# A two-layer diffusion block in fp32 on one core: GpSimd's sums go to VectorE and ScalarE, one-hots are built by fours, and the ordering pass gets new costs and slot rules

## The chip, the cores and the metric

The kernel runs on one core of a Trainium2 chip. The metric is the device time of one execution in microseconds (us), as the median of several runs. The engines are written as the profile writes them: PE (TensorE matmul), PEld (its weight loads), DVE (VectorE), ACT (ScalarE), POOL (GpSimd), SP (SyncE, which here only issues DMAs).

## The reference, cut to what matters

Two layers work on 256 latent tokens and 256 context tokens of width 1024. Each layer has a token mixer with three branches and then a feed-forward that picks 128 of 16384 experts for each token.

```python
def token_mixer(h, hc, ...):          # latent and context tokens
    qA, kA, vA, qB, kB, vB, qkvC, zC, aC, bC, gl = split_cols(h @ w_in)
    oA, oAc = diff_attention(...)     # softmax attention, difference of two maps
    oB, oBc = window_gqa(...)         # windowed attention with a sink
    oC, oCc = gated_deltanet(...)     # chunked recurrence, forward and backward
    return merge_branches((oA, oB, oC), gl, b_gate, w_branch, w_out), ...

def peer_ffn(h, wq, keys, u_tab, v_tab):
    q = (t @ wq).reshape(n, 8, 2, 128)
    s = einsum('thcd,cnd->thcn', q, keys)
    sv, si = top_k(s, 16)                          # of 128, per half
    cand = sv[:, :, 0, :, None] + sv[:, :, 1, None, :]
    cv, ci = top_k(cand, 16)                       # 16 of the sums
    eid = i1 * 128 + i2;  gw = softmax(cv)
    act = gelu(einsum('pd,ped->pe', t, u_tab[eid]))
    return einsum('pe,ped->pd', act * gw, v_tab[eid])

for l in range(2):
    m, mc = token_mixer(...)
    x = x + gt1 * m
    x = x + gt2 * peer_ffn(modulate(x, ...), ...)
    if l == 0:                                     # the context ends after layer 0
        xc = xc + gt1c * mc
        xc = xc + gt2c * peer_ffn(modulate(xc, ...), ...)
```

## The kernel before

The program isn't written in the order in which it runs. `Kern` calls methods of `Rec`, which looks like the five engines and only records operations (`Op`). `Rec.order` then plays a list schedule: it has a duration for each operation (`cost`), a priority (the place in the recording plus `base`), and pools of SBUF and PSUM slots, and it writes down in which order each engine gets its instructions. `emit` issues them in that order, so that all instructions stand at one line of the profile (L603), and groups are told apart by operation, names and shapes. Each engine then runs its own list in order.

**Slots.** Working tiles live in classes: `b4` (4 KB a partition, 36 slots), `b2` (9), `b1` (8), and 8 PSUM banks `ps`. Three tags have no slots of their own and borrow them (`BORROW`): `rows` up to 8 of `b4` and `ga` up to 3 of `b4` for the gathers below, `psg` up to 2 of `ps`. `restore` gives them back. Before the change it runs when a tile of that very tag is freed and the gathers' list is already done; the last `rows` tile is freed ahead of the list's end, the last `ga` tile at its end.

**Lanes and distance.** The gathers are recorded in lane -1, all else in lane 0. An operation that opens a tile may run ahead of the oldest unfinished one by a weighted amount of work `FAR`, and from `NEAR` on it must leave `SPARE` slots of each class free.

**Splits.** A product in fp32 accuracy is three fp32r matmuls (`mm3`): each operand is split into a rounded part (`scalar.copy`, shown as ACT CAST) and a rest (a subtraction, shown as TENSOR_TENSOR fp32r<-f32, on DVE or POOL). `WPOOL` sends half of the weight pieces of layer 0's latent mixer to POOL, `UP1` every fourth of the first 64 `u` chunks' splits of layer 1, and `VP = 8` seven of eight `v` splits of layer 1.

**Stages.** Labels are layer and stream: `01` is layer 0's context, `00` its latents, `11` and `10` the same for layer 1. In the order of time: `01` mixer; `01 front` and `01 route` (top-k of the experts, a long run of DVE instructions); then side by side the `00` mixer and the context's expert layer by gathers (`peer_gather`): `U0`, `V0`, `U1`, `V1` for the two blocks of 128 tokens. A `U` step is an indirect DMA on POOL that fetches 128 rows of 4 KB into a `rows` tile, and a DVE product with a sum (SCALAR_TENSOR_TENSOR rows<-rows,ga); a `V` step is four such DMAs and eight small matmuls. The latents' expert layer runs densely (`peer_dense`): `route`, then `build`, which makes for each token a 128x128 matrix of weights from two one-hot matrices and one matmul and stores it to HBM, 16 tokens at a time; then for each of the 128 chunks of 128 experts `dU` (24 matmuls of 256 columns, GELU) and `dV` (12 matmuls of 512 columns). `pre` is the number of `dU` chunks that are recorded ahead of the first `dV`. Layer 1 follows: `11` mixer, `10` mixer, `10 route`, `10 build`, `10 dU` and `10 dV`.

`Kern.aux` is the engine of three kinds of products in `route` (sums of candidates, and two products in `decode`): DVE in layer 0, POOL in layer 1. In the recurrence (`gdn_chains`) POOL multiplies masks and rows by a gate for each of two heads at once: `m1`, `m2` (names consts, gd_g), `vb` (gd_hb), `kd` (gd_ex), `kg` (gd_bg).

Of the kernel before, what the change touches and what calls it, by code (L numbers as in the profile page):

```python
# [20 lines left out]
KT = 8  # L21
# [22 lines left out]
WPOOL = (1, 3, 5, 7)  # L44
UP0, UP1 = (), range(0, 64, 4)
PRE1 = 64
OUTV = False
# [3 lines left out]
VP = 8  # L51
GBASE, RBASE = 0, -8000
PRE = 48
LOAD = {"tensor": 1.0, "vector": 0.3, "scalar": 0.2}
NEAR, FAR = 20.0, 150.0
# [224 lines left out]
class Rec:  # L280
# [5 lines left out]
    def __init__(self, nc, pools, bufs):  # L286
# [5 lines left out]
        self.lane, self.cw = 0, {}  # L292
# [8 lines left out]
    def cost(self, eng, meth, out, ins, kw, args):  # L301
# [27 lines left out]
        if kw.get("op") == OP.pow:
            return 0.3 + 0.165 * n, 0  # L330
        c = {"tensor_tensor": 2.2, "memset": 0.3, "tensor_copy": 3.6}.get(meth, 4.0)
        return 0.05 + n * c / 1000.0, 0

    def add(self, eng, meth, args, kw):
# [10 lines left out]
        o.dur, o.dma = self.cost(eng, meth, outs[0], ins, kw, args)  # L345
        preds = {}
# [23 lines left out]
        o.lane = self.lane  # L370
        o.cw = self.cw[o.lane] = self.cw.get(o.lane, 0.0) + o.dur * LOAD.get(eng, 0.0)
# [14 lines left out]
    def order(self):  # L386
# [55 lines left out]
        together, last_out, pe_at = {}, None, 0.0  # L442
# [13 lines left out]
        def borrow(tag):  # L456
# [4 lines left out]
            if not slots[a] or load[a][ops_at(owner[a]):].max(initial=0) > cap[a] - 1:  # L461
# [15 lines left out]
        def blocked(o):  # L477
            for t in o.tiles:
# [1308 lines left out]
```

## Time and profile before

| | |
|---|---|
| three runs | 3962.46, 3938.74, 3939.72 us |
| median | 3939.72 us |
| the profiled execution | 3933.92 us, of which its span 3932.1 us |
| mean granted TensorE clock | 0.933 of 2.4 GHz |
| busy, share of the span | PE 90%, PEld 76%, DVE 63%, ACT 41%, POOL 38% |
| HBM | 837.78 MB by DMA, 213 GB/s in the mean |

The span runs from the program's first instruction to its last. Matmul ends are modelled and matmuls overlap, so a busy PE isn't a PE at its peak, and PE's share alone doesn't say what a stage costs. Shares are means over stages with different limits; the stretches below are cut at the stages.

### The profile page before, as it was taken

Reading aid. Unit: us, or ns where it says so; the run is one execution under the profiler, and the core shown is the slowest. Engines: PE = TensorE matmul, PEld = TensorE weight load, DVE = VectorE, ACT = ScalarE, POOL = GpSimd, SP = SyncE. Lnnn points to the kernel's source line nnn. Section 1 sums busy time; section 2 is a strip of 40 time slices with the busy share of each in tenths; the row PEclk is TensorE's granted clock in tenths of the full one; section 3 lists DMA queues with packets and bytes.
Section 4 is the critical chain, followed back from the end, with each engine's and each line's share of the span. In section 5 each row is a group of like instructions: output and inputs, shape, how many; then the busy total and the mean of one; then the engine's idle time right before and its main releaser. Section 6 shows DMA issues by size and latency. Waiting matters only on the chain. (4 is left out here: it accounts for less than half of the span.)

```text
span 3932.1 us, 64402 instructions
## 1 busy us (share of the span) xinstructions
PE 3530.0 (90%) x24312; PEld 2982.5 (76%) x24312; DVE 2472.8 (63%) x5599; ACT 1610.0 (41%) x3070; POOL 1481.9 (38%) x1125
## 2 busy tenths in 40 slices
PE   7999964986997798889999999998996899899999
PEld 6787954866794467767777888877896699678998
DVE  4444579889656886897444454646559942555554
ACT  4544422433442233343333346544543343344443
POOL 1110123778364345663333202222023043675443
PEclk9999986877898999999999998988998999999999
DMA  7356742566466799999889851302351455565653
GB/s 279 112 169 239 254 168 98 184 230 233 161 206 231 252 368 376 384 409 361 334 332 333 310 195 43 103 28 89 103 197 65 129 184 170 190 222 213 221 207 142
DMA packets 300966, 837.78 MB, mean 213 GB/s; under 512 B 26736, under 2 KB 96752, under 8 KB 300656
## 3 DMA queue, kind: packets, MB, share of 16 engines
q1 hardware_dynamic: 153168, 522.80, 37.2%
q0 software_dynamic: 73728, 268.47, 18.6%
q10 hardware_dynamic: 73760, 42.40, 3.6%
q8 instruction: 192, 3.15, 0.3%
q14 instruction: 118, 0.97, 0.1%
HBM read 792.67 MB, written 40.89 MB: 212 GB/s over the span
## 5 line engine op out<-in xcount | busy, mean ns | idle before, releaser
L603 PE MATMUL ps<-b,b 128*128 128x256 f32 (+4 forms) x18528 | 2742.4, 309 | 202.7 <-DVE b L603 134.8
L603 PEld LDWEIGHTS ps<-b,b 128*128 128x128 f32 (+2 forms) x18528 | 2449.7, 192 | 476.8 <-DVE b L603 163.3
L603 DVE TENSOR_TENSOR b<-b,b 128x1024 fp32r<-128x1024 f32 (+3 forms) x1065 | 1142.8, 1106 | 817.2 <-ACT b L603 550.9
L603 ACT CAST b<-b 128x1024 fp32r<-128x1024 f32 (+1 forms) x982 | 917.4, 976 | 702.6 <-PE ps L603 297.9
L603 POOL TENSOR_TENSOR b<-b,b 128x1024 fp32r<-128x1024 f32 (+2 forms) x241 | 586.8, 2445 | 922.7 <-DVE b L603 367.5
L603 ACT COPY b<-ps 128x256 f32<-128x256 f32 (+3 forms) x896 | 291.2, 350 | 676.4 <-PE ps L603 666.6
L603 POOL DMA_INDIRECT rows<-in_u_tab,eid x256 | 357.8, 1398 | 271.1 <-DVE rows L603 118.2
L603 POOL DMA_INDIRECT rows<-in_v_tab,eidT x256 | 284.0, 1109 | 426.5 <-PE ps L603 354.6
L603 PE MATMUL ps<-b 128*128 128x128 f32 (+1 forms) x2048 | 337.9, 320 | 19.2 <-ACT b L603 7.5
L603 PE MATMUL ps<-consts,b 128*128 128x128 f32 (+1 forms) x1290 | 261.1, 316 | 103.8 <-DVE b L603 76.9
L603 ACT ACTIVATE b<-ps 128x512 f32<-128x512 f32 (+1 forms) x264 | 136.7, 520 | 523.5 <-PE ps L603 507.0
L603 PEld LDWEIGHTS ps<-b 128*128 128x128 f32 (+1 forms) x2048 | 255.7, 207 | 119.6 <-DVE b L603 39.6
L603 DVE SCALAR_TENSOR_TENSOR rows<-rows,ga 128x1024 f32<-128x1024 f32 x256 | 322.9, 1288 | 4.4 <-DMA rows<-in_u_tab,eid 2.4
L603 PEld LDWEIGHTS ps<-consts,b 128*128 128x128 f32 x1290 | 184.4, 180 | 148.2 <-issue 68.8
L603 DVE TENSOR_SCALAR b<-consts,b 128x128 f32<-128x128 f32 x1024 | 235.4, 309 | 10.8 <-DMA gd<-b 7.7
L603 PE MATMUL ps<-rows,ga 128*32 128x512 f32 x1024 | 160.5, 626 | 19.0 <-DMA rows<-in_v_tab,eidT 17.8
L603 DVE COPY_PREDICATED b<-masks,ps 128x64 f32<-128x64 uint8 (+1 forms) x416 | 83.7, 251 | 148.5 <-PE ps L603 146.9
L603 ACT COPY b<-b 128x128 f32<-128x128 f32 x384 | 108.0, 303 | 60.5 <-DVE b L603 56.1
L603 DVE TENSOR_TENSOR b<-ps,b 128x128 f32<-128x128 f32 (+4 forms) x144 | 61.9, 454 | 93.8 <-PE ps L603 57.8
L603 PEld LDWEIGHTS ps<-rows,ga 128*32 128x32 f32 x1024 | 29.5, 111 | 94.6 <-DMA rows<-in_v_tab,eidT 47.8
L603 PE MATMUL ps<-b,cs 128*32 128x256 f32 x768 | 69.8, 430 | 12.2 <-DVE cs L603 11.5
L603 ACT ACTIVATE b<-b 128x512 f32<-128x512 f32 (+1 forms) x62 | 38.9, 629 | 96.0 <-DVE b L603 42.5
(176 smaller groups left out, 1450.6 us busy)
## 6 DMA issues: line engine op xcount, KB each, us to landing
b<-in_u_cols SPq DMA_DIRECT2D x256, 512.0 KB
b<-in_v_tab SPq DMA_DIRECT2D x256, 512.0 KB
b<-in_w_in SPq DMA_DIRECT2D x184, 512.0 KB
gd<-b ACTq DMA_DIRECT2D x64, 512.0 KB
b<-gd SPq DMA_DIRECT2D x64, 512.0 KB
b<-in_w_ada SPq DMA_DIRECT2D x48, 512.0 KB
b<-in_w_ada SPq DMA_DIRECT2D x96, 256.0 KB
b<-in_wq SPq DMA_DIRECT2D x48, 512.0 KB
```

The lines of the kernel that those rows point to most:

```text
L603: r = getattr(getattr(nc, o.eng), o.meth)(*[_real(x) for x in o.args], **{k: _real(x) for k, x in o.kw.items()})
```

## The change

Constants: `WPOOL`, `UP1` become empty and `VP` 1, so that no split is on POOL; `OUTV` sends the output projection's sum to DVE, and `aux` stays DVE in layer 1. The sum in `qk_prep` goes from POOL to DVE. The five gate products of `gdn_chains` become ScalarE activations with a scale pointer, one a head. In `weights` four tokens' first one-hots are one DVE TENSOR_TENSOR with broadcast operands, and of each four second one-hots one is made by ScalarE as relu(gw - gw * |i - iota|). `order` gives all borrowed slots back when the gathers' list is done, lets `rows` borrow with a look only as far as the place where the two lists meet, has `FAR` at 80 for 150, `pre` at 32 for 48 in layer 0, leaves routing out of the distance (`URGENT = 0`), and lets layer 1's context mixer run ahead of `FAR` once the gathers are done (`FREE1`). Its cost table has new numbers, and two instructions of DVE and POOL that both read two SBUF tensors can't start at one time in its play (`port`).

```diff
-WPOOL = (1, 3, 5, 7)
-UP0, UP1 = (), range(0, 64, 4)
+WPOOL = ()
+UP0, UP1 = (), ()
-OUTV = False
+OUTV = True
-VP = 8
+VP = 1
+ACTB = (1, 1)
+TAIL, FREE1 = 0, True
+FREE = {"b4": 4, "b2": 2, "b1": 1, "ps": 0}
-PRE = 48
+PRE = 32
-NEAR, FAR = 20.0, 150.0
+NEAR, FAR, URGENT = 20.0, 80.0, 0.0
...
+        o.port = eng in ("vector", "gpsimd") and not o.dma and sum(
+            isinstance(x, V) and x.n > 1 and x.tile.kind == "sb" for x in ins) > 1
...
+                    if o.port:
+                        at = max(at, port)
+                        port = at + o.dur
...
-                if t.tag in BORROW and (not BORROW[t.tag][2] or lpos[lane] == len(lanes[lane])):
-                    restore(t.tag)
+                for tag in BORROW:
+                    if owner.get(tag) == lane and (lpos[lane] == len(lanes[lane]) or tag == t.tag and not BORROW[tag][2]):
+                        restore(tag)
...
-            nc.gpsimd.tensor_tensor(qv, qv, t1, op=OP.add)
+            nc.vector.tensor_tensor(qv, qv, t1, op=OP.add)
...
-                nc.gpsimd.tensor_tensor(m1, M1[:, None, :].to_broadcast([P, H2, P]), bc(gc), op=OP.mult)
+                for h in range(H2):
+                    nc.scalar.activation(m1[:, h], M1, AF.Copy, scale=gc[:, h:h + 1])
...
+                nc.vector.tensor_tensor(A[:, :, 0], io4, sc[:, 1, k:k + 4, None].to_broadcast([P, 4, P]), op=OP.is_equal)
                 for t in range(4):
                     k = t0 + q + t
-                    nc.vector.tensor_scalar(A[:, t, 0], self.iota, sc[:, 1, k:k + 1], None, OP.is_equal)
-                    nc.vector.tensor_scalar(A[:, t, 1], self.iota, sc[:, 0, k:k + 1], sc[:, 2, k:k + 1],
-                                            OP.is_equal, OP.mult)
+                    if t >= ACTB[l]:
+                        nc.vector.tensor_scalar(A[:, t, 1], self.iota, sc[:, 0, k:k + 1], sc[:, 2, k:k + 1],
+                                                OP.is_equal, OP.mult)
+                    else:
+                        d = A[:, t, 1]
+                        nc.scalar.activation(d, self.iota, AF.Abs, scale=-1.0, bias=sc[:, 0, k:k + 1])
+                        nc.scalar.activation(d, d, AF.Relu, scale=sc[:, 3, k:k + 1], bias=sc[:, 2, k:k + 1])
...
-        self.aux = self.nc.gpsimd
+        pass
         self.lab("1 norm1")
+        self.nc.free = FREE1
```

The change moves instructions between engines and lets the play order all of them anew. On PE the list stays close: it has the same 20928 operations, and most stages begin within some 250 places of where they began (`00 dV` and `V1` some 350 to 400 places earlier).

**POOL in the `00` mixer, beside the gathers.** In the list before, gate products of the recurrence and a weight split (the 128x1024 row) stand between the gathers' DMAs (`rows<-in_u_tab`):

```order
L603 TENSOR_TENSOR b_1647_8025<-consts_71,gd_g_7192 128x256 x2
L603 TENSOR_TENSOR b_1575_7605<-b_1468_7506,gd_hb_7171 128x256
L603 TENSOR_TENSOR b_1611_7699<-b_1467_7461,gd_bg_7252 128x256
L603 TENSOR_TENSOR b_1575_7605<-b_1467_7461,gd_ex_7241 128x256
L603 COPY b_1646_8070<-consts_71 128x256
L603 TENSOR_TENSOR b_1956_8086<-consts_71,rows_p_91 128x128 x2
L603 DMA rows_8097<-in_u_tab,eid_1303_6473 128x1024
L603 TENSOR_TENSOR b_1611_7699<-b_1468_7506,gd_hb_7171 128x256
L603 DMA rows_8117<-in_u_tab,eid_1303_6473 128x1024
L603 TENSOR_TENSOR b_1611_7699<-b_1467_7461,gd_ex_7241 128x256
L603 TENSOR_TENSOR b_1689_8137<-b_1687_7398,b_1688_7580 128x1024
L603 DMA rows_8165<-in_u_tab,eid_1303_6473 128x1024
```

In the list after, the same stretch of POOL has the DMAs and a few small rows:

```order
L625 DMA rows_8252<-in_u_tab,eid_1303_6459 128x1024
L625 DMA rows_8277<-in_u_tab,eid_1303_6459 128x1024
L625 DMA rows_8295<-in_u_tab,eid_1303_6459 128x1024
L625 COPY b_1732_8316<-consts_71 128x256
L625 TENSOR_TENSOR b_1865_8334<-consts_71,rows_p_91 128x128 x2
L625 DMA rows_8347<-in_u_tab,eid_1303_6459 128x1024
L625 DMA rows_8376<-in_u_tab,eid_1303_6459 128x1024
```

The gate products now stand on ACT between the recurrence's copies, two for each that POOL had. On DVE, 81 of the 128 sums of `U0` stand ahead of the first instruction of `00 attB1`, where 112 stood; 5 stand ahead of the end of `01 route`, where 13 stood.

**DVE and ACT in `10 build`.** DVE had eight one-hots for four tokens, on its list before:

```order
L603 TENSOR_SCALAR b_5907_31178<-consts_71,b_5777_30336 128x128 x8
L603 TENSOR_SCALAR b_5909_31196<-consts_71,b_5777_30336 128x128 x8
L603 TENSOR_SCALAR b_5911_31214<-consts_71,b_5777_30336 128x128 x8
L603 TENSOR_SCALAR b_5913_31230<-consts_71,b_5777_30336 128x128 x8
L603 TENSOR_SCALAR b_5917_31246<-consts_71,b_5777_30336 128x128 x8
```

and has four instructions for them after:

```order
L625 TENSOR_TENSOR b_5831_30687<-consts_71,b_5781_30474 128x4x128
L625 TENSOR_SCALAR b_5831_30687<-consts_71,b_5781_30474 128x128 x3
L625 TENSOR_TENSOR b_5833_30703<-consts_71,b_5781_30474 128x4x128
L625 TENSOR_SCALAR b_5833_30703<-consts_71,b_5781_30474 128x128 x3
L625 TENSOR_TENSOR b_5835_30727<-consts_71,b_5781_30474 128x4x128
```

ACT had the two copies out of PSUM for each four tokens and the two stores for each sixteen. After, the fourth one-hot's two activations stand among them, one or two groups of four ahead of the copies:

```order
L625 DMA gd_30575<-b_5809_30646 1024x1x128
L625 DMA gd_30577<-b_5810_30651 1024x1x128
L625 ACTIVATE b_5831_30687<-b_5831_30687,b_5781_30474 128x128
L625 ACTIVATE b_5833_30703<-consts_71,b_5781_30474 128x128
L625 COPY b_5819_30706<-ps_30691 128x64x4
L625 COPY b_5820_30711<-ps_30691 128x64x4
L625 ACTIVATE b_5833_30703<-b_5833_30703,b_5781_30474 128x128
L625 COPY b_5819_30706<-ps_30708 128x64x4
L625 COPY b_5820_30711<-ps_30708 128x64x4
```

**POOL in layer 1's expert layer.** Its list before has 144 splits of `u` and `v` tiles here, and ends with these rows:

```order
L603 TENSOR_TENSOR b_6969_37880<-b_6967_37776,b_6968_37871 128x1024
L603 TENSOR_TENSOR b_6972_37898<-b_6970_37794,b_6971_37877 128x1024
L603 TENSOR_TENSOR b_6985_37924<-b_6983_37828,b_6984_37906 128x1024
L1783 UNCONDITIONAL_BRANCH
L1783 ISA
```

After, its last work is the root of `10 dnorm`, ahead of the expert layer, and all splits are on DVE:

```order
L625 TENSOR_TENSOR b_5366_27987<-b_5366_27987,b_5510_28857 128x512
L625 TENSOR_SCALAR rs_29205<-rs_29205 128x2
L625 TENSOR_TENSOR rs_29205<-rs_29205,mhalf_69 128x2
L1824 UNCONDITIONAL_BRANCH
L1824 ISA
```

## Rows read from the trace of the kernel before

**Rows 1.** The page, busy us of each engine (share of the span) and instructions.
```profile
PE 3530.0 (90%) x24312; PEld 2982.5 (76%) x24312; DVE 2472.8 (63%) x5599; ACT 1610.0 (41%) x3070; POOL 1481.9 (38%) x1125
```

**Rows 2.** Busy time by stretch: us, engines, PEclk, DMA share, GB/s.
```profile
500.00:690.00 190.00, 98.86 (x740) 94.13 (x739) 166.15 (x612) 53.73 (x88) 53.53 (x40) 0.74 0.36 124
690.00:1085.00 395.00, 337.12 (x2209) 285.26 (x2209) 315.64 (x615) 158.05 (x413) 269.72 (x222) 0.80 0.61 201
...
1185.00:1480.00 295.00, 242.32 (x1520) 151.70 (x1515) 239.07 (x1045) 78.03 (x184) 133.10 (x122) 0.91 0.80 287
1480.00:1870.00 390.00, 348.27 (x2086) 294.56 (x2087) 322.29 (x482) 146.04 (x174) 212.56 (x147) 0.97 0.98 382
...
2343.00:2940.00 597.00, 562.00 (x4375) 499.57 (x4375) 328.99 (x712) 312.45 (x799) 124.38 (x154) 0.93 0.29 96
2940.00:3170.00 230.00, 181.22 (x1080) 146.69 (x1079) 219.64 (x978) 79.17 (x180) 40.05 (x53) 0.90 0.34 99
...
3340.00:3540.00 200.00, 180.98 (x747) 138.95 (x746) 107.43 (x93) 80.41 (x95) 131.27 (x52) 0.95 0.59 205
3540.00:3932.00 392.00, 383.23 (x2410) 345.11 (x2408) 201.72 (x178) 166.60 (x195) 169.96 (x61) 0.99 0.54 196
```

**Rows 3.** Whom PE waited for, whole span: us, times, longest.
```profile
PE ps L603 <- DVE b L603: 215.5, 95, 29.1
```

**Rows 4.** DVE's groups at 1870 to 2170, POOL only gathering: count, busy, mean ns.
```profile
L603 DVE TENSOR_TENSOR b<-b,b 128x1024 fp32r<-128x1024 f32 x91 | 108.4, 1223 | 82.5 <-ACT b L603 51.8 <-PE ps L603 22.0 <-issue 8.4
L603 DVE TENSOR_TENSOR b<-b,b 128x256 f32<-128x256 f32 x44 | 16.7, 422 | 62.3 <-ACT b L603 62.3
L603 DVE TENSOR_TENSOR b<-b,b 128x512 fp32r<-128x512 f32 x22 | 15.2, 690 | 11.1 <-ACT b L603 11.1
```

**Rows 5.** DVE's groups at 3340 to 3540, POOL busy with splits.
```profile
L603 DVE TENSOR_TENSOR b<-b,b 128x256 f32<-128x256 f32 x56 | 58.6, 1109 | 32.8 <-DMA b<-gd 32.8
```

**Rows 6.** The timeline at 3420 to 3428, of DVE and of POOL: start, us.
```profile
3422.60 7.51 DVE L603 TENSOR_TENSOR b<-b,b 128x256 f32<-128x256 f32 x3 [0.85 <-DMA b<-gd]
...
3422.33 7.49 POOL L603 TENSOR_TENSOR b<-b,b 128x1024 fp32r<-128x1024 f32 x3 [2.35 <-issue]
```

**Rows 7.** DVE's and POOL's groups at 690 to 1085, the latent mixer.
```profile
L603 DVE SCALAR_TENSOR_TENSOR rows<-rows,ga 128x1024 f32<-128x1024 f32 x110 | 148.8, 1382 | 0.0
L603 DVE TENSOR_TENSOR b<-b,b 128x1024 fp32r<-128x1024 f32 x20 | 32.9, 1646 | 3.5 <-PE ps L603 3.5
...
L603 POOL TENSOR_TENSOR b<-b,b 128x1024 fp32r<-128x1024 f32 x19 | 47.6, 2507 | 48.3 <-ACT b L603 48.1
```

**Rows 8.** Groups of the whole span that price the moved instructions.
```profile
L603 POOL TENSOR_TENSOR b<-b,b 128x1024 fp32r<-128x1024 f32 x191 | 505.8, 2658 | 597.0 <-PE ps L603 245.8 <-ACT b L603 227.6 <-DVE b L603 66.7
L603 DVE TENSOR_SCALAR b<-consts,b 128x128 f32<-128x128 f32 x1024 | 235.4, 309 | 10.8 <-DMA gd<-b 7.7 <-issue 1.4 <-ACT b L603 1.3
L603 ACT COPY b<-b 128x128 f32<-128x128 f32 x384 | 108.0, 303 | 60.5 <-DVE b L603 56.1 <-DVE gS L603 2.5 <-ACT b L603 1.1
L603 POOL TENSOR_TENSOR b<-consts,gd_g 128x256 f32<-128x256 f32 x56 | 39.0, 717 | 18.2 <-DVE gd_g L603 14.1 <-ACT b L603 4.1
L603 ACT ACTIVATE b<-ps,modT,A 128x256 f32<-128x256 f32 x48 | 24.3, 563 | 22.5 <-PE ps L603 20.7 <-issue 1.7
L603 ACT ACTIVATE b<-ps,cols_p 128x256 f32<-128x256 f32 x46 | 19.9, 472 | 26.2 <-PE ps L603 24.7 <-issue 1.5
```

**Rows 9.** ACT's timeline in `10 build`; ACTq is its DMA issue.
```profile
3094.03 0.65 ACT L603 COPY b<-ps 128x256 f32<-128x256 f32 x2 [1.16 <-PE ps L603]
3095.84 0.65 ACT L603 COPY b<-ps 128x256 f32<-128x256 f32 x2 [1.16 <-PE ps L603]
3096.24 1.25 ACTq L603 DMA_DIRECT2D gd<-b  x2
```

**Rows 10.** PE's groups at 3540 to 3922, the steady end of layer 1.
```profile
L603 PE MATMUL ps<-b,b 128*128 128x512 f32 x858 | 201.9, 394 | 0.8 <-POOL b L603 0.8
L603 PE MATMUL ps<-b,b 128*128 128x256 f32 x1536 | 185.0, 281 | 0.0
```

More of the change, by code (lines that the diff above doesn't have):

```diff
@@ L316, in cost @@
             return max(c * n, 140 if dt == BF else 64) / 2330.0, 0
-        big = max([n] + [x.n for x in ins if isinstance(x, V)])
-        ps = any(isinstance(x, V) and x.tile.kind == "ps" for x in list(ins) + [out])
+        vs = [x for x in ins if isinstance(x, V)]
+        big = max([n] + [x.n for x in vs])
+        ps = any(x.tile.kind == "ps" for x in vs + [out])
+        ptrs = sum(x.n == 1 for x in vs)
         if eng == "scalar":
-            ptr = any(isinstance(kw.get(x), V) for x in ("scale", "bias"))
-            return (0.05 if ps else 0.095) + (0.08 if ptr else 0.0) + big / 1200.0, 0
+            both = all(isinstance(kw.get(x), V) for x in ("scale", "bias"))
+            acc = 0.1 if kw.get("accum_out") is not None else 0.0
+            return (0.05 if ps else 0.095) + (0.19 if both else 0.09 if ptrs else 0.0) + acc + big / 1200.0, 0
@@ L322, in cost @@
         if eng == "vector":
-            two = sum(isinstance(x, V) and x.n > 1 for x in ins) < 2 and not ps and meth in (
-                "tensor_scalar", "tensor_copy", "tensor_single_scalar")
-            if meth == "tensor_tensor" and out.dt == BF and all(x.dt == BF for x in ins if isinstance(x, V)):
+            wide = [x for x in vs if x.n > 1]
+            two = len(wide) < 2 and not ps and not ptrs and meth in ("tensor_scalar", "tensor_copy", "tensor_single_scalar")
+            if meth == "tensor_tensor" and out.dt == BF and all(x.dt == BF for x in vs):
@@ L326, in cost @@
                 two = True
-            ptr = (0.11 if meth == "tensor_scalar" else 0.06) if any(isinstance(x, V) and x.n == 1 for x in ins) else 0.0
-            return (0.125 if ps else 0.065) + ptr + big / (1920.0 if two else 960.0), 0
+            base = 0.065 if not ps or len(wide) > 1 else 0.125
+            if meth in ("max_index", "match_replace") or any(x.dt in (I32, U32) for x in vs):
+                base += 0.06
+            c = base + 0.06 * bool(ptrs) + big / (1920.0 if two else 960.0)
@@ L460, in borrow @@
             a = BORROW[tag][0]
-            if not slots[a] or load[a][ops_at(owner[a]):].max(initial=0) > cap[a] - 1:
+            if not slots[a] or load[a][ops_at(owner[a]):join.get((owner[tag], owner[a]), N)].max(initial=0) > cap[a] - 1:
                 return False
@@ L490, in blocked @@
                         dist = o.cw - head.cw
-                        if dist > FAR:
+                        free = o.free and lpos[-1] >= len(lanes[-1]) - TAIL
+                        if dist > FAR and not free:
                             return "far"
-                        if dist > NEAR or o.lane != main:
-                            keep = SPARE.get(t.tag, 0)
+                        if free and dist > NEAR:
+                            keep = FREE.get(t.tag, 0)
+                        elif dist > NEAR or o.lane != main:
+                            keep = SPARE.get(t.tag, 0) + (LOADS if o.dma and t.tag == "b4" else 0)
                     if load[t.tag][front:f].max() + 1 > cap[t.tag] - keep:
```

55 lines of the change are left out of this document (34 added, 21 removed).

## The prediction

> **What bounds the kernel now.** I read the page's first part, then the busy time by stretch, then whom PE waited for, then single groups in a calm and in a crowded stretch. PE is busy for 90% of the span [rows 1], and in 3540 to 3932 for 383 of 392 us at a granted clock of 0.99 [rows 2]: there PE bounds, and nothing that other engines get can help. The change keeps every matmul, so all it can win is PE's idle time, and what PE loses at the lower of its two clock levels, 1.2 GHz. The idle time is the stretch less PE's busy time [rows 2]: 91 us in 500 to 690 (context routing), 58 in 690 to 1085 (latent mixer with the gathers), 53 in 1185 to 1480 (latent routing and `build`), 42 in 1480 to 1870 (the second `U` gathers), 35 in 2343 to 2940 (layer 1's mixers), 49 in 2940 to 3170 (its routing and `build`), 19 in 3340 to 3540 (its first `dV` chunks). That is 347 us. In the first, second, third and sixth of these DVE is busy for 80 to 95% of the stretch, and over the whole span PE waited 215.5 us for DVE alone [rows 3]. So DVE is the engine whose time counts, in the middle of the kernel, and PE at the end.
>
> **What POOL's sums cost DVE.** With POOL only gathering, DVE's 128x1024 split takes 1.223 us, the 128x512 one 0.690 and the 128x256 product 0.422 [rows 4]. With POOL on splits the same 128x256 product takes 1.109 [rows 5], and one place shows why: three POOL splits take 7.49 us and three DVE products that started 0.27 us later take 7.51 [rows 6], 2.5 each. They wait for one another, whole instruction by whole instruction. So a POOL split of some 2.5 us can hold up a two-input DVE instruction for its length, and moved to DVE it costs 1.22.
>
> **The change, part by part.** The sum is made against the profiled execution, span 3932.1 us, 3933.9 with what lies around it; the median is 5.8 above that.
>
> *Splits.* 191 POOL splits of mean 2.658 us [rows 8] become 191 DVE splits of 1.223: 234 us more for DVE, spread over four places. In 690 to 1085 POOL has 19 of them [rows 7]: with 6 sums of the projection (0.69 each) 27 us more for DVE. What DVE gets back there is 110 x (1.382 - 1.223) + 20 x (1.646 - 1.223) = 26 us from two groups alone [rows 7]; smaller forms would add to it. These cancel. But 31 of the 128 `U0` sums move behind the start of `00 attB1`, eight of them out of the context's routing: 23 x 1.38 = 32 us leave the part of the latent mixer that DVE paces, and go to the merge behind it, where PE has matmuls ready. POOL's queue there also loses the gate products that stood between the gathers' DMAs, so that a DMA no longer waits behind a product that waits for PE. I take 20 us off, because recurrence steps wait on more than DVE; from -45, the most that DVE's relief makes (32, and some 13 for the smaller forms, half of what the two groups show), to +15, if ACT's added work lengthens the recurrence (below). In 500 to 690: eight sums less and six projection sums more, -10 + 4 = -6 us; -15 to +10.
>
> *Layer 1's first `dV` chunks, 3340 to 3540.* All 52 POOL instructions [rows 2] are splits: 64 us for DVE. DVE is busy 107 there, of which 56 x (1.109 - 0.422) = 38 us is waiting [rows 4, 5]; after, 107 - 38 + 64 = 133 of 200 at most. PE's price where it doesn't wait is 201.9 / 858 = 0.235 us for a 512-column matmul [rows 10]; 747 of them are 176 us, against 200 now. The end would be PE's: -24 at most; I take -20, to 0 if the gates' loads, which DVE waited for 32.8 us there [rows 5], hold the stretch. In 3540 to 3932 the same move gains nothing, since PE is full; DVE has room (202 busy of 392).
>
> *One-hots.* DVE starts them every 235.4 / 1024 = 0.230 us [rows 8], eight for four tokens: 1.84, which is ACT's pace too, a pair of copies every 1.81 [rows 9]. After: one 512-column TENSOR_TENSOR at 0.690 [rows 4], and three at 0.230, 1.38. DVE saves 0.46 x 64 = 29 us in each layer. But ACT gets two activations of 128 columns for each four tokens. A copy of that size is 0.303; a pointer costs about 0.09 (0.563 with two against 0.472 with one) [rows 8]; so 0.39 and 0.48. With the two copies (0.65) and a quarter of two stores' issue (1.25 / 4 = 0.31) [rows 9] ACT needs 1.83. `build` then keeps its pace, with ACT in DVE's place. If activations overlap as the two copies do (0.65 for two), 1.7 is the low end, -9 us a layer; without the issue time, 1.5, -20. The high end is the slower rival. What remains is DVE's free time in `build`, good for some splits. I take -8 in 1185 to 1480 (-30 to +15).
>
> *Routing of layer 1, 2940 to 3170.* `aux` brings 48 POOL instructions to DVE: eight large ones at about 1.22 and forty of a few columns at some 0.2, 18 us, and some five splits, 6; 29 us go from one-hots. DVE at 220 of 230 gets 5 us and its waits for POOL back. Less the ACT pace of `build`: -5 (-25 to +15).
>
> *Gate products.* 144 POOL instructions (0.717 for m1 and m2 [rows 8]) become 288 ACT activations of about 0.39: 112 us more for ACT, which is 41% busy [rows 1]; 158 of 395 us in the latent mixer, 312 of 597 in layer 1's mixers [rows 2]. For one step, `kg`, `vb` and `kd` are six activations, 2.3 us, against three POOL products, 2.2 at m1's price. No gain from it, and the cover is ACT's idle half.
>
> *Slots, distance, order.* Eight `b4` slots come back in layer 1 (36 for 28), so loads start earlier. In 2343 to 2940, with 35 us idle, I take -7 (-20 to +15). In 1480 to 1870 DMA is busy 0.98 of the time at 382 GB/s [rows 2], and no instruction leaves or joins DVE: 0 (-15 to +15). `FAR` at 80 takes look-ahead away, but PE's list begins its stages nearly where it did.
>
> Sum: -6 - 20 - 8 + 0 - 7 - 5 - 20 = -66 us: 3866 for the span, 3868 for the execution, 3874 from the median. I say **3870**.
>
> **A rule that speaks against it.** The Trainium skill (ScalarE: Activation LUTs, Rules for kernel authors) says to put relu, add and mul on VectorE and not on ScalarE, and budgets about 0.3 us an activation and 0.83 ns an element, an estimate of 0.41 for 128 columns. By it ACT's group of four would be 0.65 + 0.31 + 0.82 = 1.78, so the forecast stands by it too; it is the last rival below that the rule warns of.
>
> **Rivals.** *DVE takes back what it is given.* If the moved splits land in the stretches that DVE paces, only the end gains: -20 + 5 = -15, **3925**. For it: 234 us of new DVE work; DVE at 80 to 95% there. Against: 38 us of waiting in one group of one stretch alone [rows 4, 5], and 31 sums that leave.
>
> *More than the sum.* The granted clock is 0.74 and 0.80 in 500 to 1085 and 0.90 in 2940 to 3170 [rows 2], after gaps of PE. If half of the idle time of 500 to 1480, of 2940 to 3170 and all of 3340 to 3540 goes and the clock rises with it, -(202 + 49) / 2 - 19 = -145, **3795**. Against: the context's routing is one chain of DVE instructions that the change leaves.
>
> *Slower: ACT paces `build` and the recurrence.* The place is ACT's list in `00 build` and `10 build`. The second activation reads what the first wrote, and the copies stand behind both. If they don't overlap and a group takes 2.6 instead of 1.83, 128 groups x 0.77 = +99; with the -66 above and 15 us lost in the recurrence, +48: **3988**. It decides from 2.35 a group, where 128 x 0.52 eats the sum. Against: the activations stand one or two groups ahead of their copies in ACT's order.
>
> **How the numbers follow.** The forecast 0.55, more than the sum 0.15, taken back 0.20, slower 0.10. The terms' ends, which hardly fall on one side together, give the forecast 3825 to 3929 by root of squares (45 down, 59 up); 8 in 10 over all cases is **3800 to 3932**. 1% of the median, 39 us, is what a measurement of this kernel tells from no change (its runs differ by 24). Faster by over 1%: 0.85 of the forecast and the larger case, 0.47 + 0.15 and a rest of 0.02, 0.64; slower 0.10; within 1% the remaining 0.26.
>
> **What would show it.** DVE's 128x256 product at 0.42 in every stretch, POOL busy some 750 us, PE idle in 3340 to 3540 near 0; copies of `build` about 1.8 us apart with DVE idle between; 500 to 690 unchanged. The prediction is wrong if those copies lie over 2.3 us apart, or if DVE's busy share in 690 to 1085 doesn't fall and PE still waits there.

## The result, and the profile after

| | before | after |
|---|---|---|
| median of the runs on one chip | 3939.23 us (4 runs, 3933.23 to 3962.46) | 3821.48 us (4 runs, 3814.01 to 3836.78) |
| the profiled execution's span | 3932.1 us | 3835.0 us |
| mean granted TensorE clock | 0.933 | 0.937 |

The change makes the kernel faster: the ratio is 0.9704, 95% interval 0.9656 to 0.9752, 118 us by the medians. The profiled execution of after is the slowest of its four, so its span is only 97 us below [rows 1]'s. The page after, busy us of each engine:

```profile
PE 3432.8 (90%) x24312; PEld 2947.8 (77%) x24312; DVE 2448.3 (64%) x5352; ACT 1772.5 (46%) x3618; POOL 822.3 (21%) x716
```

Beside [rows 1], POOL has lost 660 us and ACT gained 163. DVE took 191 splits of 1.22 us and is busy 24 us less. To see where the time went I cut both traces where PE finishes a stage (its last matmul, found by its place in PE's list; the first cut is the first matmul of the context's `route`): `01` mixer, context routing, `00` mixer, `00 route`, `00 build`, the rest of layer 0's dense layer, `11` and `10` mixers, `10 route`, `10 build`, the rest of layer 1. Busy time by these stretches after, with [rows 2]'s columns:

```profile
0.00:532.00 532.00, 494.24 (x3997) 406.98 (x3998) 250.06 (x544) 256.99 (x649) 49.96 (x56) 0.93 0.56 198
532.00:666.00 134.00, 64.56 (x475) 62.59 (x474) 117.07 (x533) 31.04 (x53) 17.82 (x18) 0.73 0.37 123
666.00:1140.00 474.00, 428.34 (x3253) 380.29 (x3256) 394.07 (x777) 238.79 (x580) 221.27 (x188) 0.92 0.68 234
1140.00:1312.00 172.00, 138.81 (x844) 78.23 (x836) 120.66 (x537) 42.62 (x67) 78.20 (x78) 0.93 0.76 275
1312.00:1450.00 138.00, 102.65 (x679) 75.86 (x672) 103.46 (x282) 86.65 (x249) 57.41 (x55) 0.85 0.95 318
1450.00:2313.00 863.00, 808.35 (x5146) 680.06 (x5145) 540.16 (x734) 336.91 (x411) 332.87 (x247) 0.96 0.89 335
2313.00:2879.00 566.00, 537.29 (x4335) 482.15 (x4333) 336.49 (x723) 342.34 (x923) 63.91 (x73) 0.96 0.29 96
2879.00:3018.00 139.00, 80.81 (x645) 79.58 (x646) 117.23 (x525) 42.80 (x69) 0.90 (x2) 0.79 0.23 80
3018.00:3117.00 99.00, 74.73 (x520) 67.18 (x520) 89.44 (x257) 79.42 (x245) 0.00 (x0) 0.93 0.53 153
3117.00:3825.00 708.00, 701.22 (x4431) 633.19 (x4430) 374.44 (x440) 313.79 (x376) 0.00 (x0) 1.00 0.58 203
sum 3825.00, PE 3431.00 PEld 2946.11 DVE 2443.08 ACT 1771.33 POOL 822.33; mean PE 343.10 PEld 294.61 DVE 244.31 ACT 177.13 POOL 82.23
```

The same view of before at its own boundaries:

```profile
0.00:514.00 514.00, 476.27 (x3993) 398.03 (x3994) 248.59 (x537) 233.47 (x574) 75.85 (x98) 0.97 0.60 212
514.00:661.00 147.00, 63.63 (x478) 61.08 (x478) 131.99 (x550) 34.88 (x56) 33.77 (x26) 0.71 0.33 112
661.00:1184.00 523.00, 464.34 (x3253) 407.49 (x3257) 394.89 (x713) 218.82 (x500) 353.16 (x268) 0.84 0.60 201
1184.00:1337.00 153.00, 110.10 (x666) 66.80 (x658) 116.85 (x529) 33.31 (x51) 62.56 (x56) 0.85 0.60 218
1337.00:1465.00 128.00, 118.78 (x753) 73.55 (x752) 117.94 (x513) 40.66 (x127) 61.39 (x63) 0.97 1.02 355
1465.00:2330.00 865.00, 819.61 (x5197) 676.97 (x5197) 547.95 (x747) 332.50 (x400) 355.53 (x267) 0.99 0.91 346
2330.00:2929.00 599.00, 563.01 (x4381) 500.41 (x4379) 336.99 (x721) 312.69 (x799) 125.08 (x155) 0.93 0.28 93
2929.00:3055.00 126.00, 74.45 (x572) 72.47 (x572) 108.42 (x483) 41.92 (x60) 38.81 (x55) 0.80 0.21 72
3055.00:3168.00 113.00, 108.95 (x513) 76.18 (x512) 113.00 (x501) 41.04 (x127) 1.39 (x1) 0.98 0.51 145
3168.00:3922.00 754.00, 728.93 (x4508) 647.74 (x4508) 350.96 (x304) 319.55 (x376) 374.39 (x140) 0.98 0.56 196
sum 3922.00, PE 3528.06 PEld 2980.72 DVE 2467.59 ACT 1608.85 POOL 1481.93; mean PE 352.81 PEld 298.07 DVE 246.76 ACT 160.88 POOL 148.19
```

In the table below, before and after stand with the experiments. A stage of one execution is uncertain by some 15 us: up to the `00` mixer, e3, e4, e7, e11 and e12 run the same lists as after, and their `01` mixers took 515 to 523 us against after's 532 (in e3 and e4 at a granted clock of 0.96, in after at 0.93). Work also moves across the cuts (the counts of matmuls differ), so the two sums at the bottom say more than a single stage.

| stage, us | before | after | e1 | e2 | e3 | e4 | e6 | e7 | e8 | e9 | e11 |
|---|---|---|---|---|---|---|---|---|---|---|---|
| `01` mixer | 514 | 532 | 545 | 525 | 517 | 515 | 511 | 520 | 540 | 528 | 517 |
| context routing | 147 | 134 | 142 | 141 | 134 | 134 | 147 | 134 | 133 | 133 | 134 |
| `00` mixer | 523 | 474 | 479 | 476 | 474 | 474 | 523 | 478 | 493 | 490 | 478 |
| `00 route` | 154 | 172 | 150 | 172 | 175 | 172 | 153 | 176 | 174 | 162 | 173 |
| `00 build` | 128 | 138 | 131 | 128 | 141 | 144 | 128 | 126 | 131 | 137 | 128 |
| layer 0, rest | 865 | 863 | 866 | 833 | 849 | 867 | 865 | 835 | 909 | 868 | 829 |
| `11`, `10` mixers | 599 | 566 | 617 | 627 | 603 | 562 | 618 | 581 | 570 | 606 | 587 |
| `10 route` | 126 | 139 | 139 | 146 | 154 | 143 | 132 | 138 | 140 | 140 | 138 |
| `10 build` | 113 | 99 | 98 | 113 | 96 | 99 | 124 | 104 | 98 | 98 | 116 |
| layer 1, rest | 754 | 708 | 733 | 722 | 724 | 732 | 678 | 700 | 710 | 703 | 700 |
| sum, layer 0 | 2330 | 2313 | 2314 | 2275 | 2291 | 2306 | 2328 | 2269 | 2380 | 2319 | 2260 |
| sum, layer 1 | 1592 | 1512 | 1587 | 1607 | 1577 | 1536 | 1552 | 1523 | 1518 | 1547 | 1541 |

Of the 97 us, layer 0 gives 17 and layer 1 gives 80. In layer 0 the `00` mixer gains 49 and the context's routing 13, while the `01` mixer, `00 route` and `00 build` give 46 back.

One row of the table stands out. The rest of layer 0 takes 865 or 866 us with the old planner (before, e1, e6). With the new one it takes 829 to 835 in the four kernels without one-hots on ACT (e2, e7, e11, and e12 with 834), and 849 to 909 in those with them. Why they cost something in a stage that begins after `build` wasn't settled.

Whom PE waited for, whole span after:

```profile
PE ps L625 <- DVE b L625: 221.5, 61, 45.6
PE ps L625 <- ACT b L625: 123.1, 127, 10.6
```

and before:

```profile
PE ps L603 <- ACT b L603: 55.8, 77, 3.0
```

DVE is waited for as long as in [rows 3], in fewer, longer pieces; ACT for twice as long; POOL, 27.9 us before, hardly any more. PE's idle time as a whole didn't change: the stretches less PE's busy time are 3922 - 3528 = 394 us before and 3825 - 3431 = 394 after. But that sum hides two opposite moves, because in `build` PE counts as busy while it is fed slowly.

- In the two `build` stretches PE's busy time falls by 50 us (119 + 109 to 103 + 75; `00 build` has 74 matmuls fewer inside its cut) and its idle time rises by 46 (13.3 to 59.6). Together they are only 4 us shorter.
- In all other stretches, 3681 us before and 3588 after, the idle time falls by 46 us (380.7 to 334.4). PE's busy time at the lower clock level, 1.2 of 2.4 GHz, falls from 332 to 247 us by the clock's records in the two traces. What runs at that level takes half as long at the full clock, so 85 us less of it are worth some 42 us.

So in these two executions the gain is about half idle time and half clock.

### The profile page after: what moved, and what is told of

It is laid out like the page before. It is cut to its first block, busy times and chain, and to the rows that moved or that the text cites. A ratio compares the mean times of both kernels' runs of the same rounds, so it can differ in the third digit from the quotient of the medians.

```text
span 3835.0 us, 63764 instructions
## 1 busy us (share of the span) xinstructions
PE 3432.8 (90%) x24312; PEld 2947.8 (77%) x24312; DVE 2448.3 (64%) x5352; ACT 1772.5 (46%) x3618; POOL 822.3 (21%) x716
## 4 chain that ended last, share of the span: by engine, by line
PE 77%; DVE 11%; ACT 4%; DMA 4%; issue 2%; POOL 1%; ACTq 1%; POOLq 0%; DVEq 0%
PE ps L625 77%; DVE b L625 6%; ACT b L625 4%; DMA gd<-b 2%; DVE rows L625 2%; DMA rows<-in_v_tab,eidT 1%; DVE psi L625 1%; POOL rows L625 1%; DVE psv L625 1%; ACTq L625 1%; DVE pii L625 0%; DVE pS L625 0%; DVE dst L625 0%; DVE pci L625 0%; DMA b<-in_masks 0%
## 5 line engine op out<-in xcount | busy, mean ns | idle before, releaser
L625 PE MATMUL ps<-b,b 128*128 128x256 f32 (+5 forms) x18528 | 2704.0, 307 | 205.8 <-DVE b L625 142.6
L625 DVE TENSOR_TENSOR b<-b,b 128x1024 fp32r<-128x1024 f32 (+3 forms) x1282 | 1214.7, 989 | 735.2 <-ACT b L625 542.9
L625 PE MATMUL ps<-b 128*128 128x128 f32 (+1 forms) x2048 | 285.5, 306 | 65.3 <-ACT b L625 53.4
L625 PEld LDWEIGHTS ps<-b 128*128 128x128 f32 (+1 forms) x2048 | 238.8, 206 | 118.3 <-ACT b L625 93.9
L625 PE MATMUL ps<-consts,b 128*128 128x128 f32 (+1 forms) x1290 | 245.3, 304 | 86.4 <-DVE b L625 70.2
L625 DVE SCALAR_TENSOR_TENSOR rows<-rows,ga 128x1024 f32<-128x1024 f32 x256 | 306.4, 1222 | 14.8 <-DMA rows<-in_u_tab,eid 14.7
L625 POOL TENSOR_TENSOR b<-b,b 128x512 f32<-128x512 f32 x24 | 47.7, 1987 | 325.9 <-DVE b L625 273.6
L625 DVE TENSOR_TENSOR b<-consts,b 128x512 f32<-128x512 f32 x128 | 87.6, 686 | 40.3 <-PE ps L625 25.9
L625 DVE TENSOR_SCALAR b<-consts,b 128x128 f32<-128x128 f32 x384 | 111.8, 349 | 0.0
L625 DVE TENSOR_TENSOR b<-ps,b 128x512 f32<-128x512 f32 (+4 forms) x144 | 61.8, 455 | 63.0 <-PE ps L625 43.3
```

The costliest lines, as they stand in the source:

```text
L625: r = getattr(getattr(nc, o.eng), o.meth)(*[_real(x) for x in o.args], **{k: _real(x) for k, x in o.kw.items()})
```

## The experiments

Each ratio is to the kernel before on the same chip.

**e1: the engine moves alone** (splits, gates, one-hots, `aux` on their new engines; the old planner, distances and slot rule).

```diff
-class Op: ... class Rec: ...        (after's)
+class Op: ... class Rec: ...        (before's)
-PRE = 32
-NEAR, FAR, URGENT = 20.0, 80.0, 0.0
+PRE = 48
+NEAR, FAR = 20.0, 150.0
```

> All engine moves of the change (splits, gate products, route's products, one-hots by fours), with the ordering pass, its costs and its slot rules as before. Theory (DVE is relieved of POOL's two-input sums): most of the 117 us come from here, 3939 - 80 to -110 = 3830 to 3860; the dense end of layer 1 shortens by 30 to 46 us by itself. Rival (the returned slots and the new order do it): -10 to -40, 3900 to 3930, and the dense end stays within 10 us of before.

Measured: 3918.37 against 3923.63 us, 0.9983 (0.9950 to 1.0016): no difference. The `00` mixer gains 44 us as in after, and the `01` mixer and layer 1's mixers lose 49. That the moves carry the gain by themselves fell; the rest of layer 1 is 21 us shorter, where the theory had 30 to 46 and the rival less than 10.

**e2: the new planner, slot rule and distances alone** (all operations on their old engines, old one-hots).

```diff
-WPOOL = ()
-UP0, UP1 = (), ()
-VP = 1
-ACTB = (1, 1)
+WPOOL = (1, 3, 5, 7)
+UP0, UP1 = (), range(0, 64, 4)
+VP = 8
+ACTB = (0, 0)
...
+                nc.gpsimd.tensor_tensor(m1, M1[:, None, :].to_broadcast([P, H2, P]), bc(gc), op=OP.mult)
```

> The new ordering pass, costs, distance and slot return, with every operation on the engine where it was before. Theory: 3910 to 3935, since POOL's sums still hold DVE up. Rival: 3830 to 3870; with eight more slots layer 1's dense end shortens by over 30 us although POOL still splits there.

Measured: 3896.43 us, 0.9904 (0.9874 to 0.9933). The ratio lies between the theory and the rival. The `00` mixer is as short as with the moves (476, though with some 125 fewer matmuls inside the cut), so the two gains there aren't added up; layer 1 isn't faster.

**e3: after, with the old rule for giving slots back.**

```diff
-                for tag in BORROW:
-                    if owner.get(tag) == lane and (lpos[lane] == len(lanes[lane]) or tag == t.tag and not BORROW[tag][2]):
-                        restore(tag)
+                if t.tag in BORROW and (not BORROW[t.tag][2] or lpos[lane] == len(lanes[lane])):
+                    restore(t.tag)
```

> The changed kernel, but rows' eight slots stay lost after the gathers, as before. Theory: within 10 us of the changed kernel's 3821, and its dense end (build's end to the last dV) stays near 708 us. Rival (the slots feed the dense end): 25 to 45 us slower, 3845 to 3865, dense end 735 to 755 us.

Measured: 3873.19 us, 0.9836 (0.9777 to 0.9894). Without the eight `b4` slots 1.3% of the kernel's time is lost, 65 us of layer 1 in the table. Both the theory (within 10 us) and the rival's place fell: of the 65 us, 16 are in the rest of layer 1, 37 in the mixers and 15 in `10 route`.

**e4: layer 1's splits back on POOL.**

```diff
-UP0, UP1 = (), ()
-VP = 1
+UP0, UP1 = (), range(0, 64, 4)
+VP = 8
```

> The changed kernel with layer 1's 32 u splits and 112 v splits back on POOL. Theory: the dense end loses what it won, 30 to 46 us, so 3850 to 3870. The prediction's size of this term was 20 us: 3840. Rival (slots): within 8 us of 3821.

Measured: 3842.01 us, 0.9761 (0.9707 to 0.9816). The rest of layer 1 takes 732 us, not 708: 24 us, though the intervals overlap; its PE is idle there for 25 us, after's for 7.

**e5 and e6: the new slot rule added to e1, and to the kernel before, alone** (e3's diff the other way round).

> Before's ordering pass with the engine moves, and the slot return as its one new rule. Theory now (the moves free DVE, but layer 1 can use that only with the eight slots): ratio 0.980 to 0.988, layer 1's mixers at 560 to 575 us for 617 without the slots, dense end 705 to 725. Rival (the new costs, distance and port rule are needed): 0.992 to 1.000, mixers still over 600.

> The kernel before with the slot return and nothing else. Theory now: 0.990 to 1.000, since POOL's splits hold DVE up whatever is loaded; dense end 735 to 755. Rival (the slots alone carry layer 1's part): 0.980 to 0.987, mixers near 566 and dense end near 715.

Measured: e5 3883.82 against 3941.3 us, 0.9855 (0.9819 to 0.9890); e6 3899.38, 0.9904 (0.9867 to 0.9941). The slot rule alone gives the kernel before 1%, all of it in layer 1 (40 us in the table). The ratios are those of the theories, the stages aren't: in e5 the mixers took 609 us and not 560 to 575; in e6 the mixers took 618, and the rest of layer 1 678 where at least 735 was expected. Matmuls moved across cuts there, but `10 route`, `10 build` and the rest together take 934 us in e6, with its splits on POOL, against 993 before and 946 in after and in e5. Seven of the eight combinations of the three parts now stand side by side:

| ratio to before | old engines | new engines |
|---|---|---|
| old planner, old slot rule | 1 | 0.9983 (e1) |
| old planner, new slot rule | 0.9904 (e6) | 0.9855 (e5) |
| new planner, old slot rule | not run | 0.9836 (e3) |
| new planner, new slot rule | 0.9904 (e2) | 0.9704 (after) |

The slot rule gives 0.010 to 0.013 wherever it is added. The new planner gives 0.000 with the old engines and 0.015 with the new ones; the new engines 0.002 to 0.005 with the old planner and 0.020 with the new one. These two pay only together, as far as eight programs can show it: each cell is one plan, and one group of products moved in the new plan changes the ratio by as much as 0.022 (e8 below). How much belongs to the particular plan, and which of the planner's changes matters, wasn't tested, but for one rule (e10).

**e7: no one-hots on ACT** (DVE makes four together and four singly).

```diff
-ACTB = (1, 1)
+ACTB = (0, 0)
```

> The changed kernel with all second one-hots on DVE, the first ones by fours. If ACT paces build (the prediction's 1.83 us a group of four, against 0.69 + 4 x 0.23 = 1.61 for DVE): layer 0's build falls from 139 to some 110 us and layer 1's stays at 98 to 105; in all 5 to 25 us faster, 3800 to 3816 on the scale of 3821. Rival (DVE paces it): both builds 8 to 15 us longer, 3835 to 3850.

Measured: 3802.80 us, 0.9649 (0.9614 to 0.9684), the fastest ratio of all, with `00 build` at 126 us and layer 0 44 us shorter than after, 12 of them in the `01` mixer, where the lists are the same, and 28 in the rest of layer 0. The interval overlaps after's a little.

**e8: the gate products back on POOL.**

```diff
-                for h in range(H2):
-                    nc.scalar.activation(m1[:, h], M1, AF.Copy, scale=gc[:, h:h + 1])
+                nc.gpsimd.tensor_tensor(m1, M1[:, None, :].to_broadcast([P, H2, P]), bc(gc), op=OP.mult)
...
```

> The changed kernel with the recurrence's gate products back on POOL. By the prediction's step (no gain from them): within 12 us of 3821, the two mixer stages within 8 us of 474 and 566. Rival (POOL's queue, shared with the gathers, held the recurrence): 00 mixer 20 to 45 us longer, 3845 to 3870.

Measured: 3908.89 us, 0.9922 (0.9893 to 0.9952): 144 products of 0.7 us cost 2%, more than the theory and the rival had, and nearly all of it in layer 0 (2380 for 2313). The `00` mixer loses 19 us. Most, 46 us, is lost in the rest of the dense layer, where there are no gate products. Whom PE waited for there, in e8 (1460 to 2380, which takes in the last 11 us of `build`; without them 62.5 and 18.9 us):

```profile
PE ps L625 <- ACT b L625: 64.1, 22, 17.1
PE ps L625 <- DVE b L625: 22.6, 20, 3.5
```

and after:

```profile
PE ps L625 <- ACT b L625: 29.8, 11, 10.6
PE ps L625 <- DVE b L625: 24.6, 9, 9.4
```

So the products themselves aren't what PE waits for there: with them the plan puts the later work in another order, and PE waits some 33 us more for ACT. That the order does it is argued; no run holds the order fixed.

**e9: the gate products on DVE** (e8's diff with `nc.vector`).

> The changed kernel with the 144 gate products as VectorE instructions (128x256, two heads at once), neither on GpSimd nor on ScalarE; the order is planned anew. Theory: what GpSimd's gate products cost (the run before: 0.992 against 0.970) is their place in the queue in which the gathers' DMAs stand. Then VectorE is as good a place as ScalarE but for its own work, 144 x 0.42 = 61 us of which perhaps a third is on the path: ratio 0.970 to 0.980, the end of U0 near 1050 to 1080 us and the end of layer 0's dense expert layer at 2300 to 2340. Rival: it is not the queue, but that any engine other than ScalarE adds to the chain of the recurrence (VectorE paces it): ratio 0.985 to 1.00, layer 0 ending at 2370 or later.

Measured: 3873.41 us, 0.9854 (0.9819 to 0.9888). Layer 0 ends at 2319, as the theory had it; but the ratio is the rival's, and 35 of the 41 us between the two spans are lost in layer 1. `U0` ends late again, at 1111 us (after 1052, e8 1149). In e2 it ends latest of all, at 1164, and layer 0 ends at 2275: so the end of `U0` isn't what sets layer 0's end, and the queue theory falls in that form. Layer 1's mixers in e9:

```profile
2319.00:2925.00 606.00, 572.86 (x4334) 507.16 (x4333) 359.69 (x791) 309.31 (x787) 63.26 (x73) 0.90 0.27 90
```

in e3:

```profile
2291.00:2894.00 603.00, 572.87 (x4358) 509.74 (x4356) 331.55 (x716) 341.28 (x918) 64.57 (x75) 0.92 0.28 94
```

PE is idle 33 and 30 us there, after 29; its busy time is 573 against 537 for nearly the same matmuls, at a clock of 0.90 and 0.92 against 0.96. e10 below, where only a rule of the planner is gone, has the same stage at 598 us. So what e9 loses there isn't shown to be the gate products' own cost.

**e10: after, planned without the port rule.**

```diff
-                    if o.port:
-                        at = max(at, port)
-                        port = at + o.dur
```

> The changed kernel, planned without the rule that two instructions of VectorE and GpSimd which both read two SBUF tensors can't start at one time. Theory: with the splits and the gate products gone from GpSimd, few of its instructions fall under the rule, so it moves little: ratio 0.966 to 0.975, no stage more than 15 us away from the changed kernel's. Rival: the rule is what shapes the better order: ratio 0.98 or more.

Measured: 3832.07 against 3931.34 us, 0.9739 (0.9707 to 0.9770). The rule isn't shown to matter. That no stage would move by more than 15 us fell: the `11` and `10` mixers took 598 us, 32 more than in after, and layer 0 ended at 2291, 22 earlier.

**e11: all one-hots singly on DVE, as before.**

```diff
-                nc.vector.tensor_tensor(A[:, :, 0], io4, sc[:, 1, k:k + 4, None].to_broadcast([P, 4, P]), op=OP.is_equal)
+                    nc.vector.tensor_scalar(A[:, t, 0], self.iota, sc[:, 1, k:k + 1], None, OP.is_equal)
-ACTB = (1, 1)
+ACTB = (0, 0)
```

> The changed kernel with all eight one-hots of four tokens as single VectorE instructions, as before. By the prediction's prices VectorE then needs 1.84 us for four tokens, ScalarE 0.96: VectorE has 29 us more in each layer. Theory (what the prediction said: build keeps its pace with one engine in the other's place): ratio 0.966 to 0.974, 00 build at 124 to 130 us instead of 139, 10 build at 105 to 115 instead of 98. Rival: the one-hots by fours give what they take off VectorE: ratio 0.980 or more, both builds longer than 130 and 115.

Measured: 3808.27 us, 0.9683 (0.9651 to 0.9715), with `00 build` at 128 and `10 build` at 116 us. The new one-hots gain nothing over the old in the whole; in `10 build` they gain 17 us, in `00 build` they lose 10. Why `00 build` loses is seen in PE's groups there, after:

```profile
L625 PE MATMUL ps<-b 128*128 128x128 f32 x511 | 80.8, 317 | 34.8 <-ACT b L625 24.5 <-DVE b L625 7.8 <-DVE rows L625 2.2
```

and in e11 (from 1312 on; all 512 of its `00 build`, from 1303, took 100.4 us with the same waits):

```profile
L625 PE MATMUL ps<-b 128*128 128x128 f32 x488 | 96.2, 321 | 9.4 <-DVE b L625 7.4
```

The wait for DVE is the same, and after adds 24.5 us for ACT.

**e12: e7, and layer 1's routing products back on POOL.**

```diff
-ACTB = (1, 1)
+ACTB = (0, 0)
...
+        self.aux = self.nc.gpsimd
```

> The changed kernel without ScalarE's one-hots (which alone gave 0.965) and with the three kinds of products of layer 1's routing back on GpSimd. Theory: 10 route, 126 us before and 138 to 140 with these products on VectorE, comes back to 126 to 132, as VectorE has 18 us less there; the whole 0.961 to 0.966. Rival: the 10 us are PE work of other stages that moved there, and GpSimd's large products hold VectorE's two-operand instructions: 10 route 138 or more, the whole 0.966 to 0.972.

Measured: 3797.46 us, 0.9657 (0.9630 to 0.9684), `10 route` 135 us, between the theory's 126 to 132 and the rival's 138: not told apart from e7. Three kernels without ACT's one-hots (e7, e11, e12) lie at 0.9649 to 0.9683, after at 0.9704.

## Why the prediction was right, point by point

The forecast was 3870 us within 3800 to 3932; 3821 is inside it, 49 us below the forecast and 26 above the rival "more than the sum". The direction was right; the parts were not. Term by term, beside what the stage measured (some 15 us uncertain, and with matmuls that moved across cuts):

| stage | term and its range, us | measured |
|---|---|---|
| context routing | -6 (-15 to +10) | -13 |
| `00` mixer | -20 (-45 to +15) | -49 |
| `00 route` and `00 build` | -8 (-30 to +15) | +28 |
| layer 0, rest | 0 (-15 to +15) | -2 |
| `11`, `10` mixers | -7 (-20 to +15) | -33 |
| `10 route` and `10 build` | -5 (-25 to +15) | -1 |
| layer 1, rest | -20 (-24 to 0) | -46 |
| `01` mixer | none | +18 |

Four of seven lie outside their own ranges, three faster and one slower. That the sum is inside its range is in part luck.

**What bounds.** "All it can win is PE's idle time, and what PE loses at the lower of its two clock levels": right, and both came, outside the two `build` stretches 46 us of idle time and some 42 of clock. The sum had priced the idle time alone, -66, and left the clock to the rival "more than the sum". There it needed half of the idle time of the crowded stretches to go; the result lies nearer to that rival than to the forecast. In the `00` mixer both traces have 3253 matmuls; busy time times clock is 464 x 0.84 = 390 and 428 x 0.92 = 394. 36 of its 49 us are the clock's, 13 are gaps. In layer 1's mixers 563 x 0.93 = 524 and 537 x 0.96 = 516: again mostly clock. Why the clock was granted more often there isn't settled. In `10 build` PE's busy time fell from 109 to 75 us for as many matmuls at a lower clock: before, PE counted as busy while it was fed every 1.81 us.

**The lock of DVE and POOL.** Right for the instructions, not shown for the time. DVE's 128x256 product in the whole span after:

```profile
L625 DVE TENSOR_TENSOR b<-b,b 128x256 f32<-128x256 f32 x258 | 95.7, 420 | 280.1 <-ACT b L625 280.1
```

0.42 in the mean, where [rows 5] has 1.109. In the `00` mixer the groups of [rows 7] are now:

```profile
L625 DVE SCALAR_TENSOR_TENSOR rows<-rows,ga 128x1024 f32<-128x1024 f32 x123 | 147.9, 1226 | 1.2 <-DMA rows<-in_u_tab,eid 1.1
L625 DVE TENSOR_TENSOR b<-b,b 128x1024 fp32r<-128x1024 f32 x80 | 101.2, 1284 | 10.2 <-ACT b L625 7.6 <-issue 1.4 <-PE ps L625 1.0
```

1.226 and 1.284 for 1.382 and 1.646. But it isn't shown that DVE's relief made the mixer shorter. The prediction's own sign against it came: DVE's busy share in 690 to 1085 didn't fall, it rose from 80 to 87%, with more work in the same 394 us of the stage, and PE waits for DVE there as before. Before and after, whole `00` mixer:

```profile
PE ps L603 <- DVE b L603: 34.3, 17, 7.8
PE ps L603 <- POOL b L603: 14.9, 5, 7.4
```

```profile
PE ps L625 <- DVE b L625: 31.7, 18, 8.3
```

What went is the wait for POOL, and time at the lower clock. e2, with the old splits still on POOL, has the stage as short, with some 125 matmuls fewer in it. By its time, 3925, the rival "DVE takes back what it is given" fell; in this stage DVE did take it back. The context's routing gained 13 us where 6 were taken, inside that term's range. But e1 has the same engines, and the whole gains nothing: a shorter `00` mixer (-44) went with longer mixers elsewhere, until the planner was the new one.

**Layer 1's splits.** Term -20, e4 shows 24 in the stage and 22 by the ratios: right in size, within this plan. PE's idle time in the rest of layer 1 fell from 25 to 7 us. It isn't shown beyond this plan: with the old planner and the slots, the three last stages take 934 us with the splits on POOL (e6) and 946 with them on DVE (e5).

**One-hots.** The prices were right (0.402 and 0.495 us for the two activations, 0.39 and 0.48 in the prediction; DVE's group 1.38), the pace was not. ACT's timeline in `10 build` after, start and us:

```profile
3060.37 0.62 ACT L625 COPY b<-ps 128x256 f32<-128x256 f32 x2
...
3061.28 0.64 ACT L625 COPY b<-ps 128x256 f32<-128x256 f32 x2
...
3062.65 0.62 ACT L625 COPY b<-ps 128x256 f32<-128x256 f32 x2
3063.17 0.41 ACT L625 ACTIVATE b<-consts,b 128x128 f32<-128x128 f32 x1
3063.61 0.49 ACT L625 ACTIVATE b<-b,b 128x128 f32<-128x128 f32 x1
3064.01 0.39 ACT L625 ACTIVATE b<-consts,b 128x128 f32<-128x128 f32 x1
3064.30 0.62 ACT L625 COPY b<-ps 128x256 f32<-128x256 f32 x2
3064.68 1.25 ACTq L625 DMA_DIRECT2D gd<-b  x2
...
3066.67 0.62 ACT L625 COPY b<-ps 128x256 f32<-128x256 f32 x2
```

Four groups take 3066.67 - 3060.37 = 6.30 us, 1.58 each, not 1.83: most of them overlap with what follows by about 0.1 us (0.39 long, the next starts 0.29 later). It was foretold that DVE would be idle between; it was busy for 89 of 99 us. `10 build` is 14 us shorter, more than the low end of -9 that the prediction gave to overlap. In `00 build` ACT's list did hold PE, the place that the slower rival names, by another cause than its own. ACT's issue of a store takes as long as 4.31 us in this stretch, in which the DMA engines are 0.95 busy (0.52 for most of them), and copies and activations stand behind it:

```profile
1379.37 4.31 ACTq L625 DMA_DIRECT2D gd<-b  x1
1383.73 0.40 ACT L625 ACTIVATE b<-consts,b 128x128 f32<-128x128 f32 x1 [4.68 <-issue]
```

Such issues aren't new: before had 27 in its `00 build`, 36 us together and up to 5.01, after 26 with 24 us. New is that ACT also makes one-hots on which PE waits. Net, by e7 and e11, the one-hots gained nothing and may have cost some 10 to 20 us. The Trainium skill (ScalarE: Activation LUTs, Rules for kernel authors) gave the 0.41 that the prediction worked out as an estimate; the trace agrees with 0.40 for an activation with one pointer. Its advice to use VectorE and not ScalarE for relu, add and mul fits the one-hots, where the intervals still overlap, and not the gates, by 0.9704 against 0.9854 (e9).

**Gate products: the step that failed.** "No gain from it, and the cover is ACT's idle half." The cover held: an activation took 0.40 us where 0.39 was foretold, and PE waited for ACT only 13.2 us in layer 1's mixers. But "no gain" failed: with the gates elsewhere the kernel is 2.2% (POOL, e8) and 1.5% (DVE, e9) slower. The prediction priced the products themselves, 2.3 us a step against 2.2, where the runs point to the order that the plan then finds: in e8 most of the loss lies in a stage that has no gate products, in e9 in a stage that e10, with the gates on ACT, has as long.

**Slots: the term that was mis-sized.** -7 was taken, with an end at -20. Three pairs (before and e6, e1 and e5, e3 and after) give 0.96, 1.28 and 1.32%, 38 to 52 us, all in layer 1. That PE was idle for only 35 us there [rows 2] misled me: the slots pay in PE's clock (mixers at 0.92 in e3, 0.96 in after) and behind the mixers too.

**What stays open.** Why e8's plan makes PE wait some 33 us more for ACT in the dense layer wasn't settled; gates on POOL without ACT's one-hots would tell, and wasn't run. Nor was the new planner on its own. The loss of the `01` mixer (+18) against before is mostly the clock of one execution, as the same lists took 515 to 523 us in five other kernels (but its `01 outp` begins some 950 places later in PE's list, a move that the account of the order ahead of the prediction leaves out); that of `00 route` (+18) goes with 178 matmuls more inside the cut. POOL is busy for 822 us where some 750 were foretold.

## What to carry to other kernels

Change a planner's settings together with the placement on engines that it orders: here each alone gave 0 to 0.5%, both 2%. In a kernel that is planned anew, an experiment changes the order everywhere, so look where the time went before naming a cause. When PE's idle time is small, look at the granted clock stage by stage before calling the gain bounded by it, and at stages in which PE counts as busy while it is fed slowly; look also at what a stage's list waits for in slots, which a view of engine time doesn't show. Before work goes to an idle engine, look at what its list already holds there: in `00 build` ACT's held store issues of up to 5.71 us.

## What the runs showed of the hardware that wasn't expected

- The granted clock of a stretch can differ with hardly any difference in idle time: layer 1's mixers ran at 0.96, 0.92 and 0.90 with PE idle for 29, 30 and 33 us (after, e3, e9).
- ACT's short instructions mostly start before the one ahead has ended: 0.29 us after a start of 0.39 us length, 0.40 after one of 0.49 (the timeline of `10 build` above); one of 0.41 was followed 0.44 later.
- The gate products had nearly the same busy time on ACT (37.5 + 25.5 + 22.3 + 19.3 = 105 us, 288 activations) and on POOL (39.7 + 21.4 + 21.0 + 16.9 = 99 us, 144 instructions), and 59 us on DVE. Of `m1` and `m2`, the group on ACT after, and then on POOL in e8:

```profile
L625 ACT ACTIVATE b<-consts,gd_g 128x128 f32<-128x128 f32 x112 | 37.5, 399 | 0.0
```

```profile
L625 POOL TENSOR_TENSOR b<-consts,gd_g 128x256 f32<-128x256 f32 x56 | 39.7, 729 | 9.3 <-PE ps L625 4.3 <-DVE gd_g L625 2.6 <-DVE b L625 1.8
```
